# A split-precision Strassen kernel: operand cells taken in halves, one more Strassen step in two units

## The chip, the cores and the metric

One core of one Trainium2 chip runs the whole kernel. The time is device microseconds of one execution; lower is better. The times before the change are a median of three runs.

## What is computed

The reference is a decoder block in float32 on 256 rows of width 4096: an RMS norm, one wide projection `w_in`, two mixers (causal pooling over windows 2, 4, 8, 16 and a gated width-3 convolution), a projection `w_branch` of each, sigmoid gates, an output projection `w_out`, the residual and a last RMS norm. Cut to its products:

```python
h = rmsnorm(x, norm_w)
proj = einsum('bsd,de->bse', h, w_in)
u_p, z_p, u_c, b_c, c_c, z_c, g_logit = split(proj)
y_pool = causal_multiscale_pool(u_p, pool_w, pool_scale) * silu(z_p)
y_conv = causal_gated_shortconv(u_c, b_c, c_c, conv_w, conv_b) * silu(z_c)
br = einsum('bsnc,ncd->bsnd', stack([y_pool, y_conv]), w_branch)
merged = sum(sigmoid(g_logit + gate_b) * br, axis=n)
out = rmsnorm(x + einsum('bsd,de->bse', merged, w_out), final_norm_w)
```

## The kernel before, in words

**Arithmetic.** Every float32 operand is held as two rounded values, a high and a low (the rest that the rounding left). A product is three matmuls: high by high, high by low, low by high. ScalarE (ACT) makes a high by a copy into a rounding type (`highs`, line 250). VectorE (DVE) makes a low by subtracting the high from the raw value (`lows`, line 254).

**Units and steps.** The work is cut into 32 units of 1024 output columns: `cz0`, `cb0` and so on for `w_in`, `b0_0` to `b1_3` for the two branches of `w_branch`, `o0` to `o3` for `w_out`. A unit of `w_in` or `w_out` has 16 steps, a unit of a branch 8; a step takes 256 rows of the weights, as four blocks of 128 rows by 512 columns, against 256 tokens. There are two kinds. A P step does the 8 plain products, 24 matmuls. An S step does the 7 products of Strassen's scheme, 21 matmuls; for it DVE first forms three sums of blocks in `parts`, and these are split into highs and lows too. A string at the file's head gives each unit its steps, such as `SIX5` for `o0` (line 43) and `B0_MORE` for `b0_3`, the last unit of the first of the two branches (line 50).

**The ring.** Highs and lows of the weights live in `ring`, 26 cells of 128x512. `Ring.alloc` (line 222) hands out the next n cells in a circle, and only if all n are free. A P step takes 4 cells for its highs and then 4 for its lows. An S step takes 4 highs, 4 lows, and 6 for the sums. A cell is given back when the last product that reads it has been issued. An S step takes its products in the order of `groups` (line 350): N5, M2, N3, M1 read the raw blocks 3, 0, 1, 2; N6, N7, N4 read the sums. The last step of a unit, if it is an S step, has an order of its own (`closing`).

**The other operand.** The activations' side stands split in `arena` and a few tiles of its own; one of them, `last_pair`, is the sixteenth operand. For `w_out` it is made from the merged result: `m_d` in DRAM is fetched into `sa`, `sb` or `sc`, and a `Fill` (line 826) then works in phases: for an S operand DVE forms four sums, then ACT copies the highs, then DVE subtracts the lows. A fill advances by a phase at a tick, one tick for each 6 matmuls (`pop_fill`, line 878). The fills stand in the order in which the steps of `o0` use them. If a step comes and its operand isn't ready, `run_step` forces its fill on the spot: the phases that are left are issued there, behind whatever stands in the queues of ACT and DVE already. The last quarter of `m_d`, operands 12 to 15, exists only once `b1_3`, the unit before `o0`, has been gated and transposed; that happens during `o0`.

**Order.** Everything is pinned in program order on each engine. `pump` issues the splitting of coming steps as far ahead as the ring allows, up to four steps. `tick` takes one item of the epilogue of the last unit from `queue`. When a bank of sums is finished, ACT's copy of it (`evacuate`, line 425) is issued at once. The weights come by DMA on the SP queue; the fourth block of an S step gets a second block added to it by a DMA of GpSimd (POOL), the lines `raw<-in_..` on POOL.

Of the kernel before, what the change touches and what calls it, by code (L numbers as in the profile page):

```python
# [15 lines left out]
P = 128  # L16
# [25 lines left out]
HOST = "PPBPPMMPSSSPSSSPSSS"  # L42
SIX5 = "PPPPPSPSPSPSPSPS"
EIGHT4 = "PPPPSPSPSSPSSPSS"
# [4 lines left out]
B1_FIRST = "PPSPSPSP"  # L49
B0_MORE = "PPPPSSPS"  # L50
B0_FOUR = "PPPSSPSS"
# [3 lines left out]
def hybrid_block(ctx: ExitStack, tc: tile.TileContext, x, xc, prm, rows_in, w_in, pool_w, w_branch, w_out, out):  # L55
# [194 lines left out]
    def highs(cells, src):  # L250
        for i, c in runs(cells):
            act(ring[:, c], src[:, i])
# [11 lines left out]
    class Step:  # L264
# [7 lines left out]
        def first(self):  # L272
            if self.kind == "B":
                return []

            def rounded(cells):
                self.cells = cells
                if self in steps[:2]:
                    for i in range(4):
                        if self is steps[0] and i == 0:  # L280
                            copy(ring[:, cells[0]], self.block(0)[:, 0])
                        else:
                            highs(cells[i:i + 1], self.block(i))
                elif self.kind == "S":
                    highs(cells[3:4], self.corner)
                    highs(cells[0:3], self.raw)
                else:
                    highs(cells[0:3], self.raw)
                    highs(cells[3:4], self.corner)

            return [(4, None, rounded)]

# [3 lines left out]
        def rests(self, to):  # L296
            self.lows = to
            if self in steps[:2]:
                for i in range(4):
                    if self is steps[0] and i % 2 == 0:  # L300
                        x_low(0, 1 - i // 2)
                    lows(to[i:i + 1], self.cells[i:i + 1], self.block(i))
            else:
                lows(to[0:3], self.cells[0:3], self.raw)
                lows(to[3:4], self.cells[3:4], self.corner)
            self.summed = True

        def rest(self):
            if self.kind == "P":
                return [(4, None, self.rests)] + self.mid  # L310
            if self.kind == "S":
                def added(to):
                    q, w, d = self.raw, self.corner, self.cells
                    self.lows = to
                    sub(parts[:, 0], w[:, 0], q[:, 1])
                    lows(to[3:4], d[3:4], w)
                    sub(parts[:, 1:3], q[:, 0:3:2], parts[:, 0:1].to_broadcast([P, 2, NH]))
                    self.summed = True

                def split(cells):  # L320
                    self.sum_cells, self.sum_lows = cells[0:3], cells[3:6]
                    highs(cells[0:1], parts[:, 0:1])
                    highs(cells[1:3], parts[:, 1:3])
                    lows(self.lows[0:3], self.cells[0:3], self.raw)
                    lows(cells[3:6], cells[0:3], parts)

                return [(4, None, added)] + self.mid + [(6, None, split)]
            if self.kind == "B":
                def base(cells):
                    self.cells, self.lows = cells[0:4], cells[4:8]  # L330
                    highs(self.cells, quarters(E))
                    lows(self.lows, self.cells, quarters(E))

                return [(8, lambda: self.unit.flags.get("base"), base)]

            def pooled(cells):
                self.pool_cells, self.pool_lows = cells[0:2], cells[2:4]
                q = quarters(E)[:, 2 * self.g:2 * self.g + 2]
                highs(self.pool_cells, q)
                lows(self.pool_lows, self.pool_cells, q)  # L340

            return [(4, None, self.rests), (4, lambda: self.unit.flags.get(f"pooled{self.g}"), pooled)]

# [6 lines left out]
        def groups(self):  # L350
# [19 lines left out]
            else:  # L370
# [8 lines left out]
                order = ("M2", "N3", "N4", "M1", "N7", "N5", "N6") if self.closing else (  # L379
                    "N5", "M2", "N3", "M1", "N6", "N7", "N4")  # L380
                for nm in order:
# [8 lines left out]
    class Unit:  # L390
        def __init__(self, name, src, seq, ops, epi, scaled=False, before=None, dst=None):
# [11 lines left out]
            self.main[-1].closing = self.main[-1].kind == "S"  # L403
            self.s = any(st.kind == "S" for st in self.steps)
            self.total, self.seen = {}, {}
            for st in self.main:
# [95 lines left out]
    def gap(n):  # L502
        return [None] * n
# [138 lines left out]
    def band_items(c):  # L642
# [43 lines left out]

        return [trailing] + gap(4) + [counts, leading] + gap(4) + [finished]

# [67 lines left out]
    def branch_unit(n, c):  # L756
# [23 lines left out]

        text = (B1 if c else B1_FIRST) if n else (B0, B0_FOUR, B0_FOUR, B0_MORE)[c]
        u = Unit(f"b{n}_{c}", lambda i: w_branch[n, c, i], seq_y(text), y_ops[n], epi)
# [7 lines left out]
    def out_unit(c):  # L790
# [14 lines left out]

        text = (SIX5, NINE, NINE, OUT3)[c]
        u = Unit(f"o{c}", lambda i: w_out[c, i], seq_x(text), m_ops, epi, before=start if c == 3 else None)
# [9 lines left out]
    def copy(dst, src):  # L817
        return pin(nc.vector.tensor_copy(dst, src))
# [541 lines left out]
```

## Time and profile before

| | us |
|---|---|
| median of three runs (lowest, highest) | 2347.33 (2346.90, 2347.42) |
| the profiled execution | 2347.75 |
| its span, first to last instruction | 2346.0 |
| PE busy, 10381 matmuls | 2330.4 (99%) |
| DVE busy, 2179 instructions | 2140.3 (91%) |
| ACT busy, 1924 instructions | 1544.0 (66%) |
| POOL busy | 297.6 (13%) |
| DMA, mean rate | 271 GB/s |

PE is TensorE; its matmuls are pipelined, so one is recorded as 390 ns long while the next begins some 227 ns after it. A row of the timeline gives start and length in us; where several instructions are merged (x9), the length is that of all. In brackets stands the idle time before it and who ended it.

### The profile page before, as it was taken

Reading aid. Unit: us, or ns where it says so; the run is one execution under the profiler, and the core shown is the slowest. Engines: PE = TensorE matmul, PEld = TensorE weight load, DVE = VectorE, ACT = ScalarE, POOL = GpSimd, SP = SyncE. Lnnn points to the kernel's source line nnn. Section 1 sums busy time; section 2 is a strip of 40 time slices with the busy share of each in tenths; the row PEclk is TensorE's granted clock in tenths of the full one; section 3 lists DMA queues with packets and bytes.
Section 4 is the critical chain, followed back from the end, with each engine's and each line's share of the span. In section 5 each row is a group of like instructions: output and inputs, shape, how many; then the busy total and the mean of one; then the engine's idle time right before and its main releaser. Section 6 shows DMA issues by size and latency. Waiting matters only on the chain.

```text
span 2346.0 us, 29887 instructions
## 1 busy us (share of the span) xinstructions
PE 2330.4 (99%) x10381; PEld 1928.3 (82%) x10381; DVE 2140.3 (91%) x2179; ACT 1544.0 (66%) x1924; POOL 297.6 (13%) x366
## 2 busy tenths in 40 slices
PE   9999999999999999999999999999999999999998
PEld 7888888888888888888888888888888888888886
DVE  8799999999989979979999899998999889999898
ACT  6666656666666666667666767666776666666665
POOL 0111101211101111101111111111011010011110
PEclk9999999999999999999999999999999999999999
DMA  9789977989978968968999999999899889889998
GB/s 374 246 254 293 276 235 235 281 241 289 273 222 252 274 203 256 276 201 253 291 268 287 299 286 289 280 306 276 287 264 275 283 266 295 272 241 301 289 270 287
DMA packets 204551, 636.17 MB, mean 271 GB/s; under 512 B 21488, under 2 KB 29936, under 8 KB 201584
## 3 DMA queue, kind: packets, MB, share of 16 engines
q1 hardware_dynamic: 134912, 485.42, 58.9%
q0 software_dynamic: 51840, 106.98, 25.1%
q10 hardware_dynamic: 17648, 41.87, 5.1%
q8 instruction: 81, 1.33, 0.2%
q14 instruction: 70, 0.57, 0.1%
HBM read 587.00 MB, written 25.17 MB: 261 GB/s over the span
## 4 chain that ended last, share of the span: by engine, by line
PE 96%; DVE 3%; issue 1%; DMA 1%; ACT 0%; SPq 0%; DVEq 0%; ACTq 0%
PE sums L1116 67%; PE shared L1116 27%; DVE ring L65 1%; PE shared L721 1%; PE shared L483 1%; DMA raw<-in_w_in_dram 1%; DVE parts L65 0%; DVE E L65 0%; DVE Y L77 0%; ACT ring L62 0%; DVE raw L1303 0%; PE shared L697 0%; PE shared L698 0%; PE shared L700 0%; SPq L80 0%
## 5 line engine op out<-in xcount | busy, mean ns | idle before, releaser
L1116 PE MATMUL sums<-ring,arena 128*128 128x512 f32 x6693 | 1601.0, 390 | 2.8 <-DVE ring L65 2.7
L1116 PEld LDWEIGHTS sums<-ring,arena 128*128 128x128 f32 x6693 | 1253.6, 188 | 265.2 <-DVE ring L65 5.6
L65 DVE TENSOR_TENSOR ring<-raw,ring 128x512 fp32r<-128x512 f32 (+2 forms) x979 | 1089.0, 1137 | 130.0 <-PE sums L1116 49.5
L62 ACT ACTIVATE ring<-raw 128x512 fp32r<-128x512 f32 (+2 forms) x941 | 899.7, 1016 | 101.6 <-PE sums L1116 64.9
L62 ACT ACTIVATE ring<-parts 128x1024 fp32r<-128x1024 f32 (+1 forms) x492 | 402.7, 829 | 536.7 <-DVE parts L65 474.7
L1116 PE MATMUL shared<-ring,arena 128*128 128x512 f32 x2316 | 589.6, 389 | 0.0
L1116 PEld LDWEIGHTS shared<-ring,arena 128*128 128x128 f32 x2316 | 434.6, 188 | 90.4
L65 DVE TENSOR_TENSOR ring<-parts,ring 128x1536 fp32r<-128x1536 f32 (+2 forms) x270 | 418.9, 1561 | 9.3 <-ACT ring L62 8.1
L92 POOL DMA_DIRECT2D raw<-in_w_in_dram x181 | 154.6, 854 | 1369.8 <-DMA raw<-in_w_in_dram 696.3
L65 DVE TENSOR_TENSOR parts<-raw,parts 128x1024 f32<-128x1024 f32 x238 | 289.9, 1218 | 0.0
L65 DVE TENSOR_TENSOR parts<-raw 128x512 f32<-128x512 f32 x238 | 163.3, 686 | 2.4
L65 DVE TENSOR_TENSOR J<-J 128x512 f32<-128x512 f32 (+1 forms) x90 | 78.3, 870 | 16.0 <-ACT J L62 13.2
L1116 PE MATMUL shared<-ring,side 128*128 128x512 f32 x288 | 73.1, 389 | 0.0
L62 ACT ACTIVATE J<-shared 128x512 f32<-128x512 f32 x128 | 67.9, 620 | 5.1 <-PE shared L1116 4.8
L62 ACT ACTIVATE E<-sums 128x512 f32<-128x512 f32 x76 | 42.2, 597 | 44.2 <-PE sums L1116 43.0
L1116 PE MATMUL sums<-ring,last_pair 128*128 128x512 f32 x261 | 66.4, 390 | 0.5 <-DVE ring L65 0.5
L1116 PE MATMUL shared<-ring,last_pair 128*128 128x512 f32 x252 | 63.7, 389 | 0.0
L1116 PEld LDWEIGHTS shared<-ring,side 128*128 128x128 f32 x288 | 54.1, 188 | 11.3
L92 POOL DMA_DIRECT2D raw<-in_w_out_dram x32 | 27.5, 860 | 275.6 <-DMA raw<-in_w_out_dram 142.2
L1116 PEld LDWEIGHTS sums<-ring,last_pair 128*128 128x128 f32 x261 | 48.9, 188 | 11.0 <-DVE ring L65 0.9
L92 POOL DMA_DIRECT2D raw<-in_w_branch_dram x25 | 21.4, 857 | 287.4 <-DMA raw<-in_w_branch_dram 163.0
L1116 PEld LDWEIGHTS shared<-ring,last_pair 128*128 128x128 f32 x252 | 47.3, 188 | 9.9
(142 smaller groups left out, 736.2 us busy)
## 6 DMA issues: line engine op xcount, KB each, us to landing
raw<-in_w_in_dram SPq DMA_DIRECT2D x318, 768.0 KB, 7.0
raw<-in_w_in_dram SPq DMA_DIRECT2D x326, 256.0 KB, 6.0
raw<-in_w_branch_dram SPq DMA_DIRECT2D x64, 768.0 KB, 7.3
raw<-in_w_out_dram SPq DMA_DIRECT2D x64, 768.0 KB, 7.1
raw<-in_w_in_dram POOLq DMA_DIRECT2D x181, 256.0 KB, 6.8
raw<-in_w_branch_dram SPq DMA_DIRECT2D x64, 256.0 KB, 5.6
raw<-in_w_out_dram SPq DMA_DIRECT2D x64, 256.0 KB, 5.9
E<-J POOLq DMA_DIRECT2D x30, 512.0 KB, 10.2
```

The lines of the kernel that those rows point to most:

```text
L62: return pin(nc.scalar.activation(dst, src, func, **kw))
L65: return pin(nc.vector.tensor_tensor(out=dst, in0=a, in1=b, op=op))
L92: return pin(nc.gpsimd.dma_start(dst, src, accum_op=ALU.add))
L483: pin(nc.tensor.transpose(shared(j)[:, i * T + t * P:i * T + (t + 1) * P], src[:, t, c:c + P], ident))
L721: pin(nc.tensor.matmul(o, a, b, start=(k, i) == (0, 0), stop=(k, i) == (3, 2)))
L1116: pin(nc.tensor.matmul(ps, lhs, rhs, start=n == 0, stop=n == u.total[b] - 1))
```

## The change

1. **Halves.** From the third step on, the four blocks of a step are split in two couples. A couple takes 4 cells at once (two highs, two lows), one ACT copy of 1024 and one DVE subtraction of 1024. In a P step the couples are the blocks 0, 1 and 2, 3; in an S step 0, 3 and 1, 2. The six cells of the sums are laid out as high, low, high, low, high, low.
2. **Product order.** In an S step that is followed by another S step in its unit, N4 comes before N7.
3. **Band tiles.** For the first pair of windows, the items that build band matrices with POOL and DVE are eight ticks apart in place of four.
4. **More S steps.** `o0` has seven in place of six (`SEVEN4`), `b0_3` four in place of three (`B0_FOUR`, the string of the two units before it in its branch).

```diff
-SIX5 = "PPPPPSPSPSPSPSPS"
+SEVEN4 = "PPPPSPSPSPSPSSPS"
-B0_MORE = "PPPPSSPS"
...
             def rounded(cells):
                 self.cells = cells
-                if self in steps[:2]:
-                    for i in range(4):
-                        if self is steps[0] and i == 0:
-                            copy(ring[:, cells[0]], self.block(0)[:, 0])
-                        else:
-                            highs(cells[i:i + 1], self.block(i))
-                elif self.kind == "S":
-                    highs(cells[3:4], self.corner)
-                    highs(cells[0:3], self.raw)
-                else:
-                    highs(cells[0:3], self.raw)
-                    highs(cells[3:4], self.corner)
-
-            return [(4, None, rounded)]
+                for i in range(4):
+                    if self is steps[0] and i == 0:
+                        copy(ring[:, cells[0]], self.block(0)[:, 0])
+                    else:
+                        highs(cells[i:i + 1], self.block(i))
+
+            if self in steps[:2]:
+                return [(4, None, rounded)]
+            self.cells, self.lows = [None] * 4, [None] * 4
+            return [(4, None, lambda cells: self.rounded(0, cells))]
+
+        def couple(self, half):
+            i = self.load_index
+            r, c = 3 * (i % NRAW), 3 * NRAW + i % NSUM
+            which = ((0, 3), (1, 2)) if self.kind == "S" else ((0, 1), (2, 3))
+            a, b = which[half]
+            return a, b, raw[:, r + a:r + a + 2] if b < 3 else raw[:, r + a:c + 1:c - r - a]
+
+        def rounded(self, half, cells):
+            a, b, src = self.couple(half)
+            self.cells[a], self.cells[b], self.lows[a], self.lows[b] = cells
+            act(self.two(self.cells, a, b), src)
+
+        def two(self, cells, a, b):
+            assert cells[b] == cells[a] + 1
+            return ring[:, cells[a]:cells[a] + 2]
+
+        def low(self, half):
+            a, b, src = self.couple(half)
+            sub(self.two(self.lows, a, b), src, self.two(self.cells, a, b).bitcast(F32))
...
+        def halved(self):
+            def lower(_):
+                self.low(1)
+                self.summed = True
+
+            return [(None, None, lambda _: self.low(0)), (4, None, lambda cells: self.rounded(1, cells)),
+                    (None, None, lower)]
+
+        def rest(self):
             if self in steps[:2]:
-                for i in range(4):
-                    if self is steps[0] and i % 2 == 0:
-                        x_low(0, 1 - i // 2)
-                    lows(to[i:i + 1], self.cells[i:i + 1], self.block(i))
-            else:
-                lows(to[0:3], self.cells[0:3], self.raw)
-                lows(to[3:4], self.cells[3:4], self.corner)
-            self.summed = True
-
-        def rest(self):
+                return [(4, None, self.rests)] + self.mid
             if self.kind == "P":
-                return [(4, None, self.rests)] + self.mid
+                return self.halved() + self.mid
             if self.kind == "S":
-                def added(to):
-                    q, w, d = self.raw, self.corner, self.cells
-                    self.lows = to
+                def added(cells):
+                    q, w = self.raw, self.corner
+                    self.rounded(1, cells)
                     sub(parts[:, 0], w[:, 0], q[:, 1])
-                    lows(to[3:4], d[3:4], w)
+                    self.low(0)
                     sub(parts[:, 1:3], q[:, 0:3:2], parts[:, 0:1].to_broadcast([P, 2, NH]))
                     self.summed = True
 
                 def split(cells):
-                    self.sum_cells, self.sum_lows = cells[0:3], cells[3:6]
-                    highs(cells[0:1], parts[:, 0:1])
-                    highs(cells[1:3], parts[:, 1:3])
-                    lows(self.lows[0:3], self.cells[0:3], self.raw)
-                    lows(cells[3:6], cells[0:3], parts)
+                    c, l = self.sum_cells, self.sum_lows = cells[0::2], cells[1::2]
+                    highs(c[0:1], parts[:, 0:1])
+                    highs(c[1:3], parts[:, 1:3])
+                    self.low(1)
+                    lows(l, c, parts)
 
                 return [(4, None, added)] + self.mid + [(6, None, split)]
...
-            return [(4, None, self.rests), (4, lambda: self.unit.flags.get(f"pooled{self.g}"), pooled)]
+            return self.halved() + [(4, lambda: self.unit.flags.get(f"pooled{self.g}"), pooled)]
...
-                    "N5", "M2", "N3", "M1", "N6", "N7", "N4")
+                    "N5", "M2", "N3", "M1", "N6", "N7", "N4") if self.ends else (
+                    "N5", "M2", "N3", "M1", "N6", "N4", "N7")
...
+            for i, st in enumerate(self.main):
+                st.ends = all(q.kind == "P" for q in self.main[i + 1:])
...
-        return [trailing] + gap(4) + [counts, leading] + gap(4) + [finished]
+        return [trailing] + gap(4 * (2 - c)) + [counts, leading] + gap(4 * (2 - c)) + [finished]
...
-        text = (B1 if c else B1_FIRST) if n else (B0, B0_FOUR, B0_FOUR, B0_MORE)[c]
+        text = (B1 if c else B1_FIRST) if n else (B0, B0_FOUR, B0_FOUR, B0_FOUR)[c]
...
-        text = (SIX5, NINE, NINE, OUT3)[c]
+        text = (SEVEN4, NINE, NINE, OUT3)[c]
```

What it moves, at three places. The first is DVE in `o0`, up to its last fill of `last_pair` (`ring<-raw` is a low of the weights, `ring<-parts` a low of the sums; `sa`, `sb`, `sc`, `sd` are staging tiles of the fills, `sd` a second place for the four sums). Before:

```order
L65 TENSOR_TENSOR sa<-sa,sb 128x128
L65 TENSOR_TENSOR sa<-sb 128x128
L65 TENSOR_TENSOR sa<-sb,sa 128x128
L65 TENSOR_TENSOR parts<-raw 128x512
L65 TENSOR_TENSOR ring<-raw,ring 128x512
L65 TENSOR_TENSOR parts<-raw,parts 128x1024
L65 TENSOR_TENSOR ring<-raw,ring 128x1536
L65 TENSOR_TENSOR ring<-parts,ring 128x1536
L65 TENSOR_TENSOR last_pair<-sa,last_pair 128x512
L65 TENSOR_TENSOR last_pair<-sb,last_pair 128x512
L65 TENSOR_TENSOR ring<-raw,ring 128x1536
```

And now:

```order
L64 TENSOR_TENSOR ring<-raw,ring 128x1024 x2
L64 TENSOR_TENSOR arena<-sa,arena 128x512
L64 TENSOR_TENSOR arena<-sb,arena 128x384
L64 TENSOR_TENSOR sa<-sa 128x128 x4
L64 TENSOR_TENSOR parts<-raw 128x512
L64 TENSOR_TENSOR ring<-raw,ring 128x1024
L64 TENSOR_TENSOR parts<-raw,parts 128x1024
L64 TENSOR_TENSOR ring<-raw,ring 128x1024
L64 TENSOR_TENSOR ring<-parts,ring 128x3x512
L64 TENSOR_TENSOR ring<-raw,ring 128x1024
L64 TENSOR_TENSOR last_pair<-sa,last_pair 128x512 x2
```

The splitting of one S step stood between the last four sums of a fill and the lows of `last_pair`; now the lows of another fill (`arena`), four more sums and the splitting of parts of three steps stand ahead of them.

The second place is ACT at the end of `o0`, from the last copy into `last_pair` on (`E<-sums_84` is the copy of a finished bank of sums; `arena<-sa` and the row behind it are the highs of the last step's operand). Before:

```order
L62 ACTIVATE last_pair<-sb 128x512
L62 ACTIVATE ring<-raw 128x512
L62 ACTIVATE ring<-raw 128x1024
L62 ACTIVATE ring<-raw 128x512
L62 ACTIVATE ring<-parts 128x512
L62 ACTIVATE ring<-parts 128x1024
L62 ACTIVATE ring<-raw 128x1536
L62 ACTIVATE ring<-raw 128x512
L62 ACTIVATE arena<-sa 128x512
L62 ACTIVATE arena<-sc 128x384
L62 ACTIVATE E<-sums_84 128x512
```

And now:

```order
L61 ACTIVATE ring<-raw 128x1024
L61 ACTIVATE last_pair<-sa 128x512 x2
L61 ACTIVATE ring<-raw 128x1024
L61 ACTIVATE E<-sums_84 128x512
L61 ACTIVATE ring<-raw 128x1024
L61 ACTIVATE arena<-sa 128x512
L61 ACTIVATE arena<-sc 128x512
```

The highs of the last operand stood ahead of the copy of the bank `sums_84`; now they stand behind it and behind a splitting of 1024.

The third place is DVE in `cz1`, the fifth unit, between two rows of the convolution's epilogue (`E<-J,Y`). Before:

```order
L65 TENSOR_TENSOR E<-J,Y 128x512
L65 TENSOR_TENSOR parts<-raw 128x512
L65 TENSOR_TENSOR ring<-raw,ring 128x512
L65 TENSOR_TENSOR parts<-raw,parts 128x1024
L65 TENSOR_TENSOR ring<-raw,ring 128x1536
L65 TENSOR_TENSOR ring<-parts,ring 128x1536
L65 TENSOR_TENSOR E<-J,Y 128x512
```

And now:

```order
L64 TENSOR_TENSOR E<-J,Y 128x512
L64 TENSOR_TENSOR parts<-raw 128x512
L64 TENSOR_TENSOR ring<-raw,ring 128x1024
L64 TENSOR_TENSOR parts<-raw,parts 128x1024
L64 TENSOR_TENSOR E<-J,Y 128x512
L64 TENSOR_TENSOR ring<-raw,ring 128x1024
L64 TENSOR_TENSOR ring<-parts,ring 128x3x512
```

The three-block lows of the weights have become two of two blocks, and the first of them stands ahead of the second subtraction into `parts`.

More of the change, by code (lines that the diff above doesn't have):

```diff
@@ L297, in rests @@
             self.lows = to
-            if self in steps[:2]:
-                for i in range(4):
-                    if self is steps[0] and i % 2 == 0:
-                        x_low(0, 1 - i // 2)
-                    lows(to[i:i + 1], self.cells[i:i + 1], self.block(i))
-            else:
-                lows(to[0:3], self.cells[0:3], self.raw)
-                lows(to[3:4], self.cells[3:4], self.corner)
-            self.summed = True
-        def rest(self):
+            for i in range(4):
+                if self is steps[0] and i % 2 == 0:
+                    x_low(0, 1 - i // 2)
+                lows(to[i:i + 1], self.cells[i:i + 1], self.block(i))
+            self.summed = True
+        def halved(self):
+            def lower(_):
+                self.low(1)
+                self.summed = True
+            return [(None, None, lambda _: self.low(0)), (4, None, lambda cells: self.rounded(1, cells)),
+                    (None, None, lower)]
+        def rest(self):
+            if self in steps[:2]:
+                return [(4, None, self.rests)] + self.mid
             if self.kind == "P":
-                return [(4, None, self.rests)] + self.mid
+                return self.halved() + self.mid
             if self.kind == "S":
-                def added(to):
-                    q, w, d = self.raw, self.corner, self.cells
-                    self.lows = to
+                def added(cells):
+                    q, w = self.raw, self.corner
+                    self.rounded(1, cells)
                     sub(parts[:, 0], w[:, 0], q[:, 1])
-                    lows(to[3:4], d[3:4], w)
+                    self.low(0)
                     sub(parts[:, 1:3], q[:, 0:3:2], parts[:, 0:1].to_broadcast([P, 2, NH]))
```

## The prediction

> **What bounds the kernel now.** I read the page first (span, busy times, chain that ended last), then the waits of PE, then the timeline at each of them.
>
> ```profile
> span 2346.0 us, 29887 instructions
> PE 2330.4 (99%) x10381; PEld 1928.3 (82%) x10381; DVE 2140.3 (91%) x2179; ACT 1544.0 (66%) x1924; POOL 297.6 (13%) x366
> PE 96%; DVE 3%; issue 1%; DMA 1%; ACT 0%; SPq 0%; DVEq 0%; ACTq 0%
> L1116 PE MATMUL sums<-ring,arena 128*128 128x512 f32 x6693 | 1601.0, 390 | 2.8 <-DVE ring L65 2.7
> ```
>
> PE sets the time: it is idle for 15.6 us of 2346.0. So there are two ways to change the time: the number of matmuls, and moments at which PE waits. Of the waits PE's own list has
>
> ```profile
> PE sums L1116 <- DVE ring L65: 3.2, 4, 1.3
> DVE cnt L669 <- POOL sa L657: 6.2, 4, 3.8
> ```
>
> the first row; the second, DVE's wait for POOL's band tiles, comes in below. The timeline shows where, and that there are two more too short for the list:
>
> ```profile
> 17.05 2.36 DVE L65 TENSOR_TENSOR ring<-raw,ring 128x1536 fp32r<-128x1536 f32 x2 [0.17 <-ACT ring L62]
> 18.87 3.51 PE L1116 MATMUL sums<-ring,arena 128*128 128x512 f32 x14 [1.29 <-DVE ring L65]
> 387.04 0.39 PE L1116 MATMUL sums<-ring,arena 128*128 128x512 f32 x1
> 388.17 1.43 PE L1116 MATMUL sums<-ring,arena 128*128 128x512 f32 x5 [0.75 <-DVE ring L65]
> 488.10 0.39 PE L1116 MATMUL sums<-ring,last_pair 128*128 128x512 f32 x1
> 488.98 1.43 PE L1116 MATMUL sums<-ring,last_pair 128*128 128x512 f32 x5 [0.50 <-DVE ring L65]
> 714.93 0.39 PE L1116 MATMUL sums<-ring,arena 128*128 128x512 f32 x1
> 715.99 1.43 PE L1116 MATMUL sums<-ring,arena 128*128 128x512 f32 x5 [0.68 <-DVE ring L65]
> 924.25 1.22 PE L1116 MATMUL sums<-ring,arena 128*128 128x512 f32 x3
> 925.32 0.86 PE L1116 MATMUL shared<-ring,arena 128*128 128x512 f32 x3
> 1102.35 1.11 PE L1116 MATMUL sums<-ring,arena 128*128 128x512 f32 x3
> 2049.75 6.28 PE L1116 MATMUL sums<-ring,arena 128*128 128x512 f32 x27
> ```
>
> The last row is the pace: (6.28 - 0.39) / 26 = 0.227 us from matmul to matmul. So three should take 0.84 and five 1.30. From 387.04 to 388.17 one matmul cost 1.13: 0.90 lost, and 0.13 more in the five behind it. In the same way 488 loses 0.65 + 0.13, 715 loses 0.83 + 0.13, 924 loses 0.38, 1102 loses 0.27. Sum of the five: 3.4 us. Each time it is a low that DVE delivers late.
>
> **Part 1, fewer matmuls.** An S step has 21 for a P step's 24, and two steps change: 6 x 0.227 = -1.4 us.
>
> **Part 2, halves.** DVE's and ACT's work stays what it was, nearly:
>
> ```profile
> L65 DVE TENSOR_TENSOR ring<-raw,ring 128x1536 fp32r<-128x1536 f32 x379 | 663.9, 1752 | 37.7 <-ACT ring L62 19.5 <-issue 13.9 <-PE sums L1116 2.0
> L65 DVE TENSOR_TENSOR ring<-raw,ring 128x512 fp32r<-128x512 f32 x529 | 360.3, 686 | 84.1 <-PE sums L1116 47.5 <-PE shared L1116 30.6 <-ACT ring L62 2.4
> L65 DVE TENSOR_TENSOR ring<-raw,ring 128x1024 fp32r<-128x1024 f32 x71 | 86.5, 1218 | 8.3 <-ACT ring L62 6.8 <-issue 1.5
> ```
>
> 1752 + 686 = 2438 ns against 2 x 1218 = 2436. What changes is the ring. The middle row says that DVE stood idle for 78 us because PE had not yet given cells back: the ring was full, and DVE could not work ahead. Before, the next four highs of an S step waited until four products were through (M1); now a couple is free after two, 6 matmuls or 1.4 us earlier, and in a P step after 12 matmuls of 24, 2.7 us earlier. N4 ahead of N7 frees four cells of the sums 3 matmuls (0.7 us) earlier. Each of the five waits is at most 1.0 us, so a lead that is 1.4 us longer covers it. At 488 there is a second help: DVE had waited there for POOL (up to 3.8 us, the row above), and eight ticks, 48 matmuls or 10.9 us, are more than the four ticks (5.4) and 3.8 that POOL took. I take all five as gone: -3.4 us; the bounds are -3.4 and 0. What is late next is the same row of lows, with about 0.4 us in hand.
>
> In the opening PE idles until 18.87 (1.29 us) for the three-block low that starts at 17.05; a two-block low ends 1752 - 1218 = 534 ns earlier: -0.5 us, with nothing late behind it for 24 matmuls.
>
> **Part 3, the new S steps.** Each costs DVE two subtractions into `parts` and one low of 1536 more, some 3.4 us. In `b0_3` I cost that at nothing: its string is now that of `b0_1` and `b0_2`, in whose stretches PE's list has no wait; without that cover it is 1 or 2 us. In `o0` it is the fills that count. Before, an S and a P operand alternated among the last four; now they are S, S, P, S, and an S fill has three phases. The rows for prices are those of the end of `o0` before:
>
> ```profile
> 2074.40 0.61 ACT L62 ACTIVATE last_pair<-sa 128x512 fp32r<-128x512 f32 x1
> 2074.92 0.62 ACT L62 ACTIVATE last_pair<-sb 128x512 fp32r<-128x512 f32 x1
> 2075.05 0.69 DVE L65 TENSOR_TENSOR last_pair<-sa,last_pair 128x512 fp32r<-128x512 f32 x1 [0.27 <-ACT last_pair L62]
> 2075.65 0.69 DVE L65 TENSOR_TENSOR last_pair<-sb,last_pair 128x512 fp32r<-128x512 f32 x1
> 2079.46 0.68 DVE L65 TENSOR_TENSOR parts<-raw 128x512 f32<-128x512 f32 x1
> 2080.66 1.22 DVE L65 TENSOR_TENSOR parts<-raw,parts 128x1024 f32<-128x1024 f32 x1
> 2081.03 5.60 PE L1116 MATMUL sums<-ring,last_pair 128*128 128x512 f32 x24
> 2081.80 1.82 DVE L65 TENSOR_TENSOR ring<-raw,ring 128x1024 fp32r<-128x1024 f32 x2
> 2081.98 1.06 ACT L62 ACTIVATE ring<-parts 128x1024 fp32r<-128x1024 f32 x1 [1.11 <-DVE parts L65]
> 2082.94 1.99 ACT L62 ACTIVATE ring<-raw 128x1536 fp32r<-128x1536 f32 x2
> 2083.54 1.75 DVE L65 TENSOR_TENSOR ring<-parts,ring 128x1536 fp32r<-128x1536 f32 x1
> 2085.36 0.51 ACT L62 ACTIVATE arena<-sc 128x384 fp32r<-128x384 f32 x1
> 2086.67 0.60 ACT L62 ACTIVATE E<-sums 128x512 f32<-128x512 f32 x1 [0.80 <-PE sums L1116]
> 2087.17 2.00 ACT L62 ACTIVATE ring<-raw 128x512 fp32r<-128x512 f32 x2
> ```
>
> Before, `last_pair` was ready at 2076.34 for products from 2081.03 on, 4.7 us in hand. In a row of instructions the next begins before the record of the last ends (2074.40 to 2074.92, 2075.05 to 2075.65), so a row costs start to start: ACT 0.52 for 512, 0.96 for 1024, 0.5 for a copy of a bank, an estimated 0.41 for 384; DVE 0.60, 1.14, 1.67 (1752 less the same 0.085) for 512, 1024, 1536, and 0.2 for a sum of 128. The full record counts where another engine takes over.
>
> *First operand (14th step).* I start at the sixth matmul of the 13th step, which gives back the cells that the sums of the 14th wait for (+0.39, its record, and 0.04 to hand over). From there ACT has, in its order, a copy of the sums 0.52, raw 0.96, the fill's highs 0.52 and 0.41, raw 1.07: 3.91. DVE then has a low of 1024 that waits for it, 1.14, and the fill's low 0.69: done at 5.8. PE comes to it 18 matmuls after the start, at 4.1: late by 1.7.
>
> *Second (15th step, `last_pair`).* DVE goes on from 5.7: fill 0.47 (384), four sums 0.8, parts 0.60, low 1.14, parts 1.22, which ends at 9.9. ACT copies the sums (1.06 to 11.0), DVE makes their lows (1.67), one low of the next unit (1.14), and the two of `last_pair` (0.60 + 0.69): 15.1. PE comes to it 39 matmuls after the start, at 8.8: late by 6.3 in all, 6.4 with the restart.
>
> *Third (16th step).* Its highs stand on ACT behind the copy of the bank that the 15th step's last matmul closes: 0.43 + 0.50 + 0.96 + 0.52 + 0.62 = 3.0 after that matmul, where PE would go on after 0.23: 2.8 lost. Its low ends 0.7 later where two matmuls cover 0.45, with the restart 0.4 more: 3.2. Nothing hides this one, since the copy can't start earlier.
>
> The loads are not in this path:
>
> ```profile
> raw<-in_w_out_dram SPq DMA_DIRECT2D x64, 768.0 KB, 7.1
> ```
>
> SP's loads and POOL's additions wait for lows that now come up to 6 us later, but they are issued three to four steps ahead, over 15 us, and land in 7.
>
> Together +9.6 us. The bounds: 3.2 (the queues run far enough ahead for the first two) and 12 (each of some 13 rows of DVE in the path at its full record, and the first highs 1.2 later).
>
> [...]
>
> **The sum.** -1.4 - 3.4 - 0.5 + 9.6 = +4.3. The profiled execution took 2347.75 (span 2346.0 and 1.75 around it), 0.4 above the median of 2347.33; on the median that is 2351.6. A measurement of this kernel can tell 0.2% from no change, 4.7 us: the line lies at 2352.0, within the error of my largest term.
>
> **Rivals.**
>
> *The clock falls* in `o0`.
>
> ```profile
> 5.80:2334.80 2329.00, 2325.69 (x10360) 1925.01 (x10358) 2135.08 (x2165) 1539.57 (x1917) 296.89 (x360) 1.00 0.90 271
> 2334.80:2336.80 2.00, 0.03 (x1) 0.00 (x0) 1.83 (x6) 0.80 (x4) 0.00 (x0) 1.00 1.01 414
> 2336.80:2338.80 2.00, 0.00 (x0) 0.00 (x0) 1.67 (x8) 1.29 (x3) 0.00 (x0) 0.56 0.49 199
> 1.13 4.91 PE L943 MATMUL shared<-warm 128*128 128x256 bf16 x23 [1.13 <-DVE warm L939]
> ```
>
> The granted clock (third number from the end) held through waits of 1.5 us, and fell about 2.2 us after PE's last matmul. Here PE would wait 2.8 us, do two matmuls, wait 1.6, and later 2.8 again. At the start the 23 small matmuls took 0.21 each at 256 columns, half of the later pace, for 4.9 us. So a fall costs up to 2.4 us: 2354.0, or 2356.4 for two. [...] Chance 0.2.
>
> *The operands are in time* (the other side). If ACT and DVE reach the last three fills over 6.4 us sooner than I place them, which needs that the 14th step's sums do not wait for the sixth matmul of the 13th, and the last copy is short, only the gains are left: 2347.3 - 5.3 = 2342.0. Against it: the ring holds that copy back by its order. Chance 0.06.
>
> *Only the third wait stays*, 3.2 us, or the first two come out at half: 2345 to 2348.5. Chance 0.14.
>
> *The old five stay*, since the ring isn't what DVE lacks there: 2351.6 + 3.4 = 2355.0. Against it speak the 78 us. Chance 0.1.
>
> **How the numbers follow.** My own case has 0.5, with a spread of 1.3 around 2351.6; a little under half of it lies above 2352.0. Slower: 0.2 + 0.1 + 0.2 = 0.5. Faster 0.06. The rest, 0.44, is no change. The range leaves out the case on the other side, the lower end of the partial one and two falls: 2347.5 to 2355.2.
>
> **What would show it.** After: no wait of PE on DVE between 20 and 1900 us; PE's list with waits near 2070 to 2085 only, on `arena` and `last_pair`, in sum 9 to 10 us, three of them over 1.5; a copy `E<-sums` at the last one's foot; six matmuls fewer. I am wrong if `o0` shows less than 5 us of waits, or if waits stand in the first half.

## The result and the profile after

| | us |
|---|---|
| before, median of six runs (lowest, highest) | 2347.83 (2346.90, 2348.63) |
| after, median of six runs (lowest, highest) | 2356.71 (2355.26, 2357.65) |
| ratio, with its 95% interval | 1.0038 (1.0028 to 1.0048) |
| the profiled execution of after, and its span | 2357.65, 2355.9 |

The change makes the kernel slower by 8.9 us. The prediction said 2351.6, at most 2355.2.

The page of after, in three of the lines that answer to those of before: the span, the busy times, the largest group of matmuls.

```profile
span 2355.9 us, 29761 instructions
PE 2334.3 (99%) x10375; PEld 1930.9 (82%) x10375; DVE 2154.2 (91%) x2113; ACT 1559.2 (66%) x1895; POOL 304.1 (13%) x368
L1140 PE MATMUL sums<-ring,arena 128*128 128x512 f32 x6663 | 1614.6, 390 | 3.8 <-ACT arena L61 2.7
```

There are six matmuls fewer, and yet PE is busy 3.9 us longer: some matmuls got slower. PE's list of waits (engine, tile and line waited for: us in total, times, longest) has new names in it:

```profile
PE shared L1140 <- DVE arena L64: 3.3, 1, 3.3
PE sums L1140 <- ACT arena L61: 2.7, 1, 2.7
PE sums L1140 <- ACT last_pair L61: 1.7, 1, 1.7
PE sums L1140 <- DVE last_pair L64: 1.4, 1, 1.4
PE sums L1140 <- DVE ring L64: 1.1, 2, 0.8
```

The first four lie in `o0` and are the fills of the last three operands. The last row has two waits: the opening, and one that stayed in the middle. The timeline of after at the opening and at three of the five places of the middle:

```profile
16.47 2.01 ACT L61 ACTIVATE ring<-raw 128x1024 fp32r<-128x1024 f32 x2 [2.52 <-DMA raw<-in_w_in_dram]
17.56 2.36 DVE L64 TENSOR_TENSOR ring<-raw,ring 128x1024 fp32r<-128x1024 f32 x2 [0.30 <-ACT ring L61]
18.84 1.43 PE L1140 MATMUL sums<-ring,arena 128*128 128x512 f32 x5 [0.76 <-DVE ring L64]
387.01 1.52 PE L1140 MATMUL sums<-ring,arena 128*128 128x512 f32 x6
715.83 0.84 PE L1140 MATMUL sums<-ring,arena 128*128 128x512 f32 x3
921.58 0.39 PE L1140 MATMUL sums<-ring,arena 128*128 128x512 f32 x1
922.31 0.73 PE L1140 MATMUL sums<-ring,arena 128*128 128x512 f32 x2 [0.34 <-DVE ring L64]
```

Near 387 and 715 the matmuls run on at their pace (six in 1.52, three in 0.84), and near 488 as well. Near 922 a wait stays: 0.73 for one matmul is 0.50 lost. In the opening the matmul behind the wait starts at 18.84, where it started at 18.87: the low is shorter, but it starts 0.5 later (17.56 for 17.05), since ACT's copy ahead of it waited for its load until 16.47 (15.53 before). This holds for this one execution: in the nine variants below that have the halves, the same matmul starts at 17.51 to 17.97.

The end of `o0` in after (steps 14 to 16; start, length, what it is, and the idle time before it):

```profile
2071.43 0.62 ACT L61 ACTIVATE arena<-sa 128x512 fp32r<-128x512 f32 x1
2073.12 2.35 DVE L64 TENSOR_TENSOR ring<-raw,ring 128x1024 fp32r<-128x1024 f32 x2
2075.39 0.68 DVE L64 TENSOR_TENSOR arena<-sa,arena 128x512 fp32r<-128x512 f32 x1
2076.12 0.79 PE L1140 MATMUL shared<-ring,arena 128*128 128x512 f32 x1 [3.29 <-DVE arena L64]
2078.29 1.06 ACT L61 ACTIVATE ring<-raw 128x1024 fp32r<-128x1024 f32 x1 [3.94 <-PE sums L1140]
2079.27 2.76 PE L1140 MATMUL shared<-ring,arena 128*128 128x512 f32 x6
2082.68 0.86 PE L1140 MATMUL shared<-ring,arena 128*128 128x512 f32 x3
2084.03 1.13 ACT L61 ACTIVATE last_pair<-sa 128x512 fp32r<-128x512 f32 x2
2085.22 0.73 PE L1140 MATMUL sums<-ring,last_pair 128*128 128x512 f32 x2 [1.69 <-ACT last_pair L61]
2087.36 5.29 PE L1140 MATMUL sums<-ring,last_pair 128*128 128x512 f32 x22 [1.42 <-DVE last_pair L64]
2092.69 0.60 ACT L61 ACTIVATE E<-sums 128x512 f32<-128x512 f32 x1 [1.61 <-PE sums L1140]
2094.13 0.62 ACT L61 ACTIVATE arena<-sa 128x512 fp32r<-128x512 f32 x1
2095.32 4.10 PE L1140 MATMUL sums<-ring,arena 128*128 128x512 f32 x9 [2.67 <-ACT arena L61]
2099.26 1.99 PE L1140 MATMUL shared<-ring,arena 128*128 128x512 f32 x8
```

Two things are to be seen. First the waits: from the start of one matmul to the start of the next, less 0.227, PE loses 3.46, 1.85, 1.59 and 2.83, together 9.7 us. Second the rows behind them: x6 in 2.76 and x9 in 4.10, where before six took 1.52. From 2076.71 to 2079.27 six matmuls took 2.56, which is 0.427 us from matmul to matmul, 0.2 more than the pace. The stretches of 3.41 us show why (from:to, length, then PE busy, weight loads, DVE, ACT and POOL, each with its count, then the granted clock, DMA share, GB/s):

```profile
2071.91:2075.32 3.41, 0.92 (x4) 0.33 (x3) 3.41 (x4) 2.44 (x4) 0.00 (x0) 1.00 0.89 276
2075.32:2078.73 3.41, 2.61 (x6) 2.13 (x7) 3.38 (x9) 0.44 (x1) 0.00 (x0) 0.50 0.57 194
2078.73:2082.15 3.42, 3.42 (x9) 2.65 (x9) 2.75 (x3) 1.28 (x3) 0.85 (x1) 0.50 0.73 240
2082.15:2085.56 3.41, 1.73 (x8) 1.06 (x7) 2.35 (x2) 3.01 (x4) 0.00 (x0) 1.00 0.91 226
2092.39:2095.80 3.41, 0.74 (x4) 0.30 (x2) 1.02 (x2) 2.58 (x4) 0.00 (x0) 1.00 0.57 187
2095.80:2099.21 3.41, 3.41 (x9) 2.48 (x8) 3.15 (x4) 1.19 (x2) 0.84 (x1) 0.50 0.63 175
```

The clock fell to half twice, for 6.83 and 3.41 us. From 2076.12 to 2082.68 PE did 16 matmuls in 6.56 us, 2.9 more than the pace; from 2095.32 to 2099.26 nine in 3.94, 1.9 more. Together 4.8 us.

The account, span against span (2355.9 - 2346.0 = +9.9): fewer matmuls -1.4; the five places of the middle -2.7 (the three first gone, 922 dearer by 0.2, 1102 cheaper by 0.1); the opening 0; the four waits +9.7; the half clock +4.8; the stretch behind the last matmul -0.8 (10.35 for 11.18; it is 10.34 to 10.37 in every variant with the halves and 11.27 in the one without, and why was not followed further). That is +9.6; the rest is short gaps.

### The profile page after: what moved, and what is told of

The parts are those of the page before. It is cut to its first block, busy times and chain, and to the rows that moved or that the text cites. A ratio compares the mean times of both kernels' runs of the same rounds, so it can differ in the third digit from the quotient of the medians.

```text
span 2355.9 us, 29761 instructions
## 1 busy us (share of the span) xinstructions
PE 2334.3 (99%) x10375; PEld 1930.9 (82%) x10375; DVE 2154.2 (91%) x2113; ACT 1559.2 (66%) x1895; POOL 304.1 (13%) x368
## 3 DMA queue, kind: packets, MB, share of 16 engines
q8 instruction: 81, 1.33, 0.2%
## 4 chain that ended last, share of the span: by engine, by line
PE 95%; DVE 2%; DMA 1%; ACT 1%; issue 1%; SPq 0%; ACTq 0%; DVEq 0%
PE sums L1140 66%; PE shared L1140 27%; PE shared L745 1%; DVE ring L64 1%; PE shared L507 1%; DMA sb<-m_d 1%; DMA raw<-in_w_in_dram 1%; ACT ring L61 0%; DVE E L64 0%; DVE parts L64 0%; DVE arena L64 0%; DVE raw L1327 0%; PE shared L721 0%; ACT arena L61 0%; PE shared L722 0%
## 5 line engine op out<-in xcount | busy, mean ns | idle before, releaser
L64 DVE TENSOR_TENSOR ring<-raw,ring 128x1024 fp32r<-128x1024 f32 (+1 forms) x908 | 1088.3, 1215 | 80.3 <-ACT ring L61 70.8
L61 ACT ACTIVATE ring<-raw 128x1024 fp32r<-128x1024 f32 (+1 forms) x907 | 917.9, 1049 | 175.0 <-PE sums L1140 93.2
L61 ACT ACTIVATE ring<-parts 128x512 fp32r<-128x512 f32 (+1 forms) x497 | 403.9, 823 | 461.1 <-DVE parts L64 369.4
L1140 PE MATMUL shared<-ring,arena 128*128 128x512 f32 x2340 | 616.2, 390 | 3.3 <-DVE arena L64 3.3
L1140 PEld LDWEIGHTS shared<-ring,arena 128*128 128x128 f32 x2340 | 440.2, 188 | 95.2 <-DVE arena L64 3.7
L64 DVE TENSOR_TENSOR ring<-parts,ring 128x1536 fp32r<-128x1536 f32 (+2 forms) x271 | 424.1, 1574 | 37.3 <-ACT ring L61 26.7
L61 ACT ACTIVATE J<-shared 128x512 f32<-128x512 f32 x128 | 72.9, 605 | 3.5 <-PE shared L1140 1.2
```

The source lines that it names most:

```text
L61: return pin(nc.scalar.activation(dst, src, func, **kw))
L64: return pin(nc.vector.tensor_tensor(out=dst, in0=a, in1=b, op=op))
L1140: pin(nc.tensor.matmul(ps, lhs, rhs, start=n == 0, stop=n == u.total[b] - 1))
```

## The experiments

All times are medians of five or eleven runs; before was timed again with each group, at 2347.67 (first four), 2347.81 (next four) and 2347.46 (last two). A trace shows a single execution of a variant; where that one lies at an end of its runs, the text says so.

### Six S steps in `o0`, the rest of the change kept

```diff
-        text = (SEVEN4, NINE, NINE, OUT3)[c]
+        text = ("PPPPPSPSPSPSPSPS", NINE, NINE, OUT3)[c]
```

> The halves, the product order, the band tiles and the fourth S step in b0_3 as after; o0 has its six alternating S steps again. Theory (the four waits at the end of o0 come from the last fills: the operands of steps 14 to 16 with S, S, P, S behind the splitting queue, and the two clock falls follow from those waits): the lost 9.7 us of PE's four waits and the 5.2 us lost at half clock go but for one wait of at most 2 us at the last step (the copy of the bank), the mid gain of 2.4 us and the shorter tail stay: 2344 to 2346, faster than before, no half clock before the last matmul. Rival A (the halves themselves take the time, whatever o0's string is): 2353 to 2357. Rival B (seven S steps cost half, the halves half): about 2350, with one of the two falls of the clock left.

Measured: 2344.80, ratio to before 0.9989 (0.9980 to 0.9998). One wait is left, at the last step:

```profile
PE sums L1140 <- ACT arena L61: 1.6, 1, 1.6
```

In its timeline the wait stands behind the copy of the bank:

```profile
2082.32 0.60 ACT L61 ACTIVATE E<-sums 128x512 f32<-128x512 f32 x1 [1.61 <-PE sums L1140]
2082.81 1.03 ACT L61 ACTIVATE arena<-sa 128x512 fp32r<-128x512 f32 x2
2083.90 2.44 PE L1140 MATMUL sums<-ring,arena 128*128 128x512 f32 x8 [1.62 <-ACT arena L61]
```

No half clock before the last matmul: the granted clock was 1.00 in every stretch from 1990 to 2090, and 0.999 over the span. So the halves, the product order and the rest are worth 2.9 us, and the seventh S step in `o0` costs 11.9. The wait that stays is the one forecast as the third: the fill's copies stand on ACT behind the copy of the bank. Before has no wait at this place, so these 1.8 us come with the rest of the change and not with the seventh S step.

### Three S steps in `b0_3` again, seven in `o0`

```diff
-        text = (B1 if c else B1_FIRST) if n else (B0, B0_FOUR, B0_FOUR, B0_FOUR)[c]
+        text = (B1 if c else B1_FIRST) if n else (B0, B0_FOUR, B0_FOUR, "PPPPSSPS")[c]
```

> All as after, but b0_3 has its three S steps again, and three matmuls more. Theory (the fourth S step there costs nothing but saves 0.7 us): after + 0.7, 2357.0 to 2357.5, the waits in o0 unchanged to 0.1 us. Rival (DVE's extra 3.4 us in b0_3 push work into later units): after - 1 to - 3, with waits in o0 shorter by that.

Measured: 2351.47, 1.0017 (1.0008 to 1.0025), 5.2 below after. Neither expectation holds. The first and the last wait stay, the two on `last_pair` are gone:

```profile
PE shared L1140 <- DVE arena L64: 3.2, 1, 3.2
PE sums L1140 <- ACT arena L61: 2.7, 1, 2.7
```

The waits lie far behind `b0_3`: 21 steps stand between its last one and the 14th of `o0`. What the fourth S step moved is the fetch of `m_d` for `last_pair`, first in this variant, then in after:

```profile
2057.33 0.33 ACTq L85 DMA_DIRECT2D sc<-m_d  x1
2069.09 0.29 DVE L64 TENSOR_TENSOR sd<-sc 128x128 f32<-128x128 f32 x1
```

```profile
2062.73 0.33 ACTq L85 DMA_DIRECT2D sa<-m_d  x1
2076.46 1.01 DVE L64 TENSOR_TENSOR sa<-sa 128x128 f32<-128x128 f32 x4
```

The fetch goes out 5.4 us later in after, and its four sums start 7.4 us later, behind the fill before it. Whether that is a matter of ticks or of work is the question of the variant with half a tick, below.

### Seven S steps alone, on the kernel before

```diff
-        text = (SIX5, NINE, NINE, OUT3)[c]
+        text = ("PPPPSPSPSPSPSSPS", NINE, NINE, OUT3)[c]
```

> The kernel before with the seven S steps in o0 alone: three-block splitting, old product order, b0_3 with three. Theory (the backlog of the queue is the seventh S step's own: S, S at the 14th and 13th step and an S fill in three phases): the waits at the end of o0 are of the same kind, 7 to 11 us in all with one or two falls of the clock, and the five short waits of the middle stay: 2354 to 2361. Rival A (the halves make the backlog, since each couple's low follows its own copy and ACT and DVE take turns): waits under 4 us, no fall of the clock, 2346 to 2350. Rival B (the three-block lows of an S step are worse): over 12 us of waits and over 2361.

Measured: 2357.11, 1.0040 (1.0027 to 1.0052). The longest waits:

```profile
PE sums L1116 <- ACT arena L62: 3.6, 1, 3.6
PE shared L1116 <- DVE arena L65: 1.7, 1, 1.7
```

Waits of 7.0 us at the end of `o0` and one fall of the clock, of 6.83 us (granted 0.50 from 2091.34 to 2098.17). The seventh step costs 9.4 us here, without any halves, and 11.9 with them; so the halves are not the cause of most of it.

### Seven S steps that alternate with P steps

```diff
-        text = (SEVEN4, NINE, NINE, OUT3)[c]
+        text = (SEVEN3, NINE, NINE, OUT3)[c]
```

> As after, but o0's seven S steps alternate with P steps (PPPSPSPSPSPSPSPS): the same number of matmuls and of fills, and the four last operands are P, S, P, S as before the change. Theory (what costs is two S steps in a row whose fills and splitting stand in one queue ahead of last_pair, not their number): at most one wait of 2 us at the last step, no fall of the clock before the last matmul: 2343 to 2346. Rival (the seventh S step's DVE work as such, some 3.4 us plus 2.5 of the fill, exceeds what DVE has free in o0): waits of 4 to 8 us and at least one fall, 2350 to 2356.

Measured: 2359.59, 1.0051 (1.0037 to 1.0065). My theory of two S steps in a row falls: here none stand in a row, and it is the slowest of all. The rival's sign holds, its 2356 was too little. The first S step comes one step sooner, and the waits start sooner: the first near 2022, five in `o0` in all. The granted clock was 0.50 from 2084.64 to 2088.05 and on to 2091.47, and 0.996 over the span. The longest on PE's list:

```profile
PE sums L1140 <- ACT last_pair L61: 3.8, 1, 3.8
```

### The last fills forced one step earlier

```diff
         while not st.op.ready:
             pop_fill(st.op)
+        k = u.steps.index(st)
+        if u is names["o0"] and 11 <= k < 15:
+            while not u.steps[k + 1].op.ready:
+                pop_fill(u.steps[k + 1].op)
```

> As after, with seven S steps in o0 and four in b0_3, but from the 12th step of o0 on the fill of the next step's operand is forced one step earlier, so that on ACT and DVE it stands ahead of the splitting of one whole step and, for the last, ahead of the copy of the bank. Theory A (the waits come from the place of the fills in the queues, three of them forced at the moment of need; the work itself has room): the wait at the 14th step falls from 3.46 us to under 1, the last one from 2.83 to under 0.5, no fall of the clock before the last matmul, 2343 to 2347. Theory B (DVE has too much work between the landing of the last quarter and the end of the unit, wherever the fills stand): the waits move to the rows of the ring, their sum stays at 7 us or more, 2352 to 2357.

Measured: 2348.48, 1.0001 (0.9992 to 1.0010): 8.2 of the 8.9 us are back, but it lies above the first theory's 2347. The wait at the 14th step is gone. What is left in the trace, which is of the slowest of eleven runs (2349.32), is 1.0, 1.8 and 1.6 lost at the 15th and 16th step, and one fall of 3.41 us (granted 0.50 from 2087.47 to 2090.88). The first row is the whole stretch, the second the 3.41 us ahead of the fall, with the waits of 1.8 and 1.6 in it:

```profile
2066.00:2090.00 24.00, 20.10 (x81) 15.58 (x81) 23.82 (x36) 14.74 (x22) 1.70 (x2) 0.95 0.67 203
2084.06:2087.47 3.41, 0.73 (x2) 0.30 (x2) 3.41 (x5) 3.41 (x6) 0.00 (x0) 1.00 0.86 229
```

DVE is busy for 23.82 of 24 us. So both theories seem to have a share: the place of the fills in the queues first, and behind it DVE's work, which the variant with less of it tests below.

### Half a tick

```diff
+            if u is names["b1_3"] and st is u.steps[0]:
+                state["mm"] += 3
```

> As after, but the count of matmuls from which ticks are made is put forward by three, half a tick, at the start of b1_3; no instruction is added or taken away. Without the fourth S step in b0_3 the time fell by 5 us, though that step stands 16 steps away from the waits. Theory A (it mattered only since 21 matmuls are three and a half ticks: it shifts all later fills by half a tick, after which a fetch goes out one round sooner and last_pair is in time): 2350 to 2352.5, with the waits of the variant with three S steps in b0_3, 3.4 and 2.8 us. Theory B (b0_3's fourth S step leaves ACT or DVE behind by its own work): as after, 2355 to 2357.5.

Measured: 2352.74, 1.0021 (1.0012 to 1.0030), 4.0 below after, with no instruction added or taken away. It lies 0.2 above the first theory's range. The waits on `last_pair` are gone again, and the two long ones are those of the variant with three S steps:

```profile
PE shared L1140 <- DVE arena L64: 3.3, 1, 3.3
PE sums L1140 <- ACT arena L61: 2.7, 1, 2.7
```

The fetch for `last_pair` goes out at 2058.74 and its sums start at 2070.50, at the same place among the products as with three S steps. So of the 5.2 us that `b0_3`'s fourth S step cost, some 4 came through its length: 21 matmuls are three and a half ticks, and every fill behind it is advanced at other products. The trace is of the slowest of eleven runs (2355.49; they begin at 2348.88); it also has 1.65 us of waits near 785 to 791, and its granted clock over the span was 0.996, where the variant with three S steps has 0.997.

### Six S steps, and the last fill ahead of the copy

The first variant with

```diff
+        if u is names["o0"] and st is u.steps[14]:
+            while not u.steps[15].op.ready:
+                pop_fill(u.steps[15].op)
```

> Six S steps in o0 as in the variant that was fastest so far, all else as after, and at the 15th step the fill of the 16th step's operand is forced, so that its highs stand on ACT ahead of the copy of the bank. Theory (the 1.78 us that are left at the last step come from that place alone): the wait is gone, 2344.8 - 2.0 = 2342.8, 2342.3 to 2343.5. Rival (the forced copies delay the splitting of the next unit's first steps): a wait of 0.5 to 2 us shortly after 2084 and no gain, 2344 to 2346.

Measured: 2343.25, 0.9981 (0.9973 to 0.9990): faster than both kernels, by 4.6 and 13.5 us. Of the wait of 1.6 there is left

```profile
PE sums L1140 <- DVE arena L64: 0.3, 1, 0.3
```

### A longer wait at the same place

The first variant with two more copies of 512 in front of the last wait:

```diff
-                    act(o.view[:, 0, 0:4], four)
+                    for _ in range(3 if o is names["o0"].steps[-1].op else 1):
+                        act(o.view[:, 0, 0:4], four)
```

> Six S steps in o0 as in the variant that was fastest so far, all else as after, but the copy of four of the last operand's highs is made three times in place of once, which puts two ACT rows of 0.52 us in front of the last wait and nothing else. PE's gap there was 2.00 us start to start with no fall of the clock; now it should be 3.04. Theory A (a gap of some 3 us makes the clock fall, as the two gaps of 3.06 and 3.69 after the change did, and costs eight matmuls at half pace, 1.6 us): 2344.8 + 1.04 + 1.6 = 2347.4, with matmuls at 0.427 us behind the gap. Theory B (the fall needs the waits before it, in sum over 6 us within 25): 2344.8 + 1.04 = 2345.8, no matmul at 0.427.

Measured: 2347.96, 1.0001 (0.9992 to 1.0010), 3.2 above the first variant. Its timeline at the wait:

```profile
2083.06 2.36 ACT L61 ACTIVATE arena<-sa 128x512 fp32r<-128x512 f32 x4
2085.47 4.12 PE L1141 MATMUL sums<-ring,arena 128*128 128x512 f32 x9 [2.94 <-ACT arena L61]
```

The 3.41 us ahead of the fall, in which PE was busy for 0.56:

```profile
2082.62:2086.03 3.41, 0.56 (x2) 0.30 (x2) 1.67 (x3) 3.35 (x6) 0.00 (x0) 1.00 0.52 168
```

The copies took 2.36 in place of 1.03, 1.33 more (I had put 1.04), and nine matmuls then took 4.12. A single wait of 2.94 brought a fall (granted 0.50 from 2086.03 to 2089.44): 3.2 less 1.3 is some 1.8 us for one fall. Its eleven runs lie between 2345.87 and 2350.46, where the first variant's lie between 2344.48 and 2346.62: it seems that not every execution falls alike, but only one has a trace.

### Less work for DVE, the rows where they were

The variant with the fills forced earlier, with lows of 24 columns in three steps:

```diff
-                    lows(l, c, parts)
+                    if self.unit is names["o0"] and self.unit.steps.index(self) in (10, 12, 13):
+                        for i in range(3):
+                            sub(ring[:, l[i], 0:24], parts[:, i, 0:24], ring[:, c[i], 0:24].bitcast(F32))
+                    else:
+                        lows(l, c, parts)
```

> As the variant of seven S steps with the fills forced one step earlier (2348.5), but the lows of the three sums in the 11th, 13th and 14th step of o0 are written for 24 of 512 columns, so DVE has some 4 us less to do ahead of the last two operands and every row stands where it stood; the output of o0 lacks those lows. That variant still has 4.4 us of waits at the 15th and 16th step and one fall of the clock, with DVE busy without a break from 2066 to 2090. Theory (what is left there is DVE's work: the seventh step's 3.4 us of splitting, and PE 0.7 us sooner): the waits fall to under 1 us in sum and the clock stays: 2342 to 2343.5. Rival (ACT's order, or the landing of the quarter of m_d, holds the last two fills): the waits stay at 3 to 4.4 us, 2346.5 to 2348.5.

Measured: 2343.03, 0.9982 (0.9974 to 0.9991), 5.5 below the variant it was made from, and no sign of half clock ahead of the last matmul: the granted clock over the span was 0.999, as with six S steps (0.998 in the one it was made from). In `o0` one wait is left:

```profile
PE sums L1144 <- DVE arena L64: 0.8, 1, 0.8
```

Each of the three rows of lows became 0.4 us long in place of 1.8. So what was left with the fills in front is DVE's work. Only the time is of use here, since the lows are missing.

### Six S steps with the last fill ahead, three in `b0_3`

The string of `b0_3` as in the second experiment, on top of the fastest variant.

> Six S steps in o0 with the last fill forced ahead of the copy (2343.25, the fastest so far), and three S steps in b0_3 as before the change: three matmuls more. Theory A (with the last fills in time the fourth S step of b0_3 is worth its three matmuls and nothing else): 2343.25 + 0.7 = 2343.9, no wait over 0.6 us in o0. Theory B (half a tick more shifts the fills and a wait of 1 to 3 us comes back, or b0_3's extra splitting had cost something): 2345 to 2347, or below 2343.

Measured: 2344.63, 0.9988 (0.9979 to 0.9997). That is 1.4 above the fastest where 0.7 was expected and 2345 was the rival's least; the profile has no wait over 0.3 us in `o0`. The three matmuls account for 0.7; the other 0.7 is not found and stays open. The trace can't show it: it is of the fastest of the eleven runs (2343.84), and the fastest run with four is 2343.02. So the lower ends lie 0.8 apart, near the 0.7, and the rest is in a wider spread (up to 2346.22, where four reach 2344.03).

## Why the prediction was wrong

**The forecast step that failed is the clock.** "The clock falls" stood as a rival with a chance of 0.2. That chance was an estimate: before showed only that the clock held at 1.00 through waits of up to 1.5, and no run had shown what a wait of 2.8 does. Both long waits (3.46 and 2.83) brought a fall, and with two falls that rival gave 2356.4; 2356.71 was measured. Without the 4.8 us of half clock the profiled execution's 2357.65 would be 2352.9, where the sum's +4.3 on before's 2347.75 gives 2352.1. That a wait of this size is enough by itself is shown by the variant with the longer wait (2.94). The waits of 2.8 us or more behind which the clock is shown all came with a fall: these three, 3.4 and 2.8 with three S steps in `b0_3`, 3.8 with seven S steps alone, 4.0 with the alternating ones.

**The first operand** was to be 1.7 late and was 3.46. The chain was started at the sixth matmul of the 13th step, as if ACT and DVE stood waiting for it. They were behind: ACT's highs were done at 2072.05 (2071.43 + 0.62), and the fill's low began only at 2075.39, behind two lows of the ring. DVE had no idle time to catch up in, before as little as after; busy time in 31 us, before and then after:

```profile
2046.00:2077.00 31.00, 31.00 (x139) 25.66 (x138) 30.63 (x44) 21.03 (x29) 2.58 (x3) 1.00 0.88 249
```

```profile
2046.00:2077.00 31.00, 27.71 (x121) 22.59 (x120) 30.69 (x43) 19.39 (x25) 2.55 (x3) 0.97 0.87 258
```

DVE had 30.63 of 31 us in use already. The 78 us of idle DVE that the prediction counted for the five waits are a sum over the kernel; none of them were here. A first wait of 1.7 alone would probably have brought no fall: lone waits of 1.78 (six S steps) and 1.83 (alternating) brought none, the granted clock stayed at 1.00. But two of 1.80 and 1.59 that lay in one stretch of 3.41 us did (fills forced earlier), while 1.85 and 1.59 in after, which lay in two, did not. The second operand was forecast as such a pair, 2.8 and 1.6.

**The second and third.** Forecast 4.7 and 3.2, measured 3.44 (1.85 + 1.59) and 2.83. The third is as described, at the foot of the copy `E<-sums` (2092.69, then the splitting, then the fill at 2094.13, then PE at 2095.32). The sum of all the waits, 9.6, was met by 9.7, but by errors that cancel.

**The reason given for them was wrong in part.** The prediction said that S and P operands alternated among the last four before and that it was now S, S, P, S. But the form of a fill belongs to the operand's place, not to the step: all four of the last quarter are filled with sums, before and after (in the trace of before, too, `last_pair` has its four sums, from 2068.09 on, and serves a P step). What the seventh S step adds is its own splitting, 0.60 + 1.14 + 1.67 = 3.4 us of DVE, while PE comes 0.7 sooner: 4.1 together. With the fills in front (of the six, the last one alone), six S steps leave 0.45 us of waits at the end of `o0` and seven leave 4.4, which is 3.9 more; and taking some 4 us from DVE left 0.9 of them. The other half of the waits in after is the place of the fills: forced at the moment of need, they stand behind splitting that itself waits for cells that PE gives back (ACT idle for 3.94 until 2078.29 while `last_pair` stood behind it in the queue).

**`b0_3` at nothing** was wrong. Its own work costs nothing that was found, but its length moves the ticks by a half, and in after that cost some 4 us, more than twenty steps later. No row of before that is shown here prices this; the order of the instructions far downstream, beside that of a variant with three, would have shown the fetch move.

**The five waits**: -3.4 forecast, -2.7 measured; the mechanism holds for the first three, the wait at 922 stayed. **The opening**: -0.5 forecast, 0 in the trace of after, where the load came late. It is no miss: the matmul starts at 18.87 and 18.50 in the two traces without the halves, and at 17.51 to 17.97 in nine of the ten with them. **Behind the last matmul** the halves gave 0.8, for which the sum had no term. **Six matmuls**: -1.4, as counted. The first variant bears the halves out: 2.9 us faster than before, fewer matmuls included.

**The prices of rows held.** In after, too, DVE's next row starts ahead of the end of the last: the lows x2 from 2073.12 take 2.35, and the next starts at 2075.39, 0.08 before their end, as the 0.085 of before.

**The rivals.** "Operands in time" (2342.0) did not come about; six S steps with the last fill in front (2343.25) come near its number. "The old five stay" fell: three are gone.

## What to carry to other kernels

Price a late operand from the state of the queue in that stage, not from the event that it formally waits for: an engine that is busy for 30.6 of 31 us there has no slack, whatever its average says. Here the waits of PE of 2.8 us or more behind which the clock is shown, and once two shorter ones close together (1.80 and 1.59), came with a fall of the clock to 0.50, which cost another 1.8 to 2.9 us where it was counted. So a forecast with such waits needs the fall in its main case. And where work is paced by a counter, a step that changes the count moves everything behind it: compare the order far downstream before calling the step free.

## What the runs showed of the hardware

The clock changed on a grid of 3.41 us. In after the two falls began 20.48 us apart (2075.32 and 2095.80), six times 3.413, and from the end of the second (2099.21) to the fall behind the last matmul (2348.38) are 249.17 us, 73 times 3.413. Ahead of the last matmul the half clock lasted one or two such cells of the grid, never a part of one, in each fall that is shown from end to end: 6.83 and 3.41 us in after, 3.41 twice with three S steps in `b0_3`, 3.41 with the fills forced earlier and with the longer wait. It followed a cell in which PE was busy for 0.92 and 0.74 us in after, in the variant with the longer wait 0.56; it did not follow the cell with 1.73 (2082.15 above). The shortest idle time in a cell that brought a fall is in the variant with three S steps in `b0_3`:

```profile
2073.86:2077.27 3.41, 1.43 (x6) 1.21 (x7) 3.41 (x6) 0.39 (x2) 0.00 (x0) 1.00 0.71 262
```

PE was busy for 1.43 of 3.41 here, and the next cell ran at half (0.50 from 2077.27 to 2080.68). Of the cells at full clock behind which the clock is shown, those with PE busy for 0.56 (longer wait), 0.73 (three S steps in `b0_3`, and fills forced earlier), 0.74 and 0.92 (after), 0.91 (seven alone), 1.23 (alternating) and 1.43 us were followed by half clock, and those with 1.73 and 1.99 (after), 1.75 (alternating) and 1.76 (seven alone) were not. So in these traces the line lies between 1.43 and 1.73 us of busy time, a little under half a cell. At half clock a cell with 2.61 busy (2075.32 in after) did not bring the clock back; the next, busy throughout, did (1.00 from 2082.15). Whether a wait of 3 us fills enough of one cell may differ from run to run, which would fit the eleven runs between 2345.87 and 2350.46; only one of them has a trace, so this is not shown.
